# Staging more weights in the second pass of an input projection, and moving half of a weight transform into a later stage

## The chip, the cores and the metric

One Trainium2 (trn2) chip, one of its cores. The metric is the device time of one execution in microseconds (us). TensorE is called PE (PEld its weight loads), VectorE DVE, ScalarE ACT, GpSimd POOL, SyncE SP. DMAs are issued from SP's queue and from ACT's queue.

## The reference

One layer of a bidirectional encoder block, 2048 tokens of 1024 channels, all in float32:

```python
h = rmsnorm(x, g_mix)
p = h @ w_in                                    # 512 Fourier columns, 3 x 512 Hyena columns
y_f = rmsnorm(fourier_mix(p[..., :512]), g_fourier)
y_h = rmsnorm(hyena_mix(p[..., 512:], ...), g_hyena)   # short convolution of 3, two gated long ones
x = x + concat([y_f, y_h]) @ w_out
a = square(relu(rmsnorm(x, g_mlp) @ w_fc1))     # 1024 -> 4096
x = x + a @ w_fc2                               # 4096 -> 1024
out = rmsnorm(x, g_final)
```

## The kernel before

**Products.** Each float32 operand is split into a high part (a cast, on ACT) and a low part (the difference, on DVE or POOL): `split`, lines 178 to 185. A product is then three matmuls (`mm3`, lines 187 to 191): high by high (L189), high by the weights' low part (L190), low by high (L191). The MLP is computed with seven products of half size instead of eight (Strassen's scheme in Winograd's form), `m1` to `m7`; for that, four of the operands on w_fc2's side are sums or differences of its quarters.

**The order of the work.** The kernel is written as one program for all engines. A scheduler places each engine's instructions in a fixed order beforehand: what comes earlier in the program goes first, and an instruction that is ready by its estimates may be placed ahead of earlier ones that aren't. At run time each engine and each queue keeps that order, and an instruction that waits holds what stands behind it. This holds for a DMA too: it waits in its queue, SP's or ACT's, until its buffer is free.

**The input projection, two passes** (`project`, L308). The 16 tiles of tokens (128 tokens each) go through w_in twice, each time for two groups of 512 columns (`sets`). The first pass makes two Hyena groups. It loads x (`fetch`, into buffers with the tag "xt", 2 of 1024 columns), transposes each tile on PE, splits it and writes the transposed tile to a scratch tensor `xtd` (L335). The second pass (`uf` given) makes the Fourier group and the third Hyena group. It reads the tiles from `xtd` (L339) with a DMA on SP's queue, splits them into `xh` and `xl`, and multiplies: 24 matmuls for each of the two groups, 48 per tile. The Fourier result goes to `uf` (L368, ACT), the Hyena result through the short convolution (L374 and L393 on DVE, L397 and L401 on POOL) and out to `gd` (L394, SP).

`weights_in` (L291) brings in the 16 slices of weights of a pass, 8 of each group, 128 x 512 each: load into a staging buffer (L300), split into `wh` and `wl`. In the second pass the staging buffers are the four with the tag "st". The slices of the first group come from the scratch tensor `wfd` and their low parts are made by DVE and POOL in turns (L182); those of the second group are scaled by `g_mix` and their low parts are made by DVE (L185).

**What runs beside the second pass** (`tables`, L1260, taken in turns with `project`, one step per tile). It loads tables for later stages, among them `ff`, two tiles of which use the tag "xt" and four the tag "st". And it makes the sums of w_fc2 (`second_weights`, L1244): for each of 16 pairs of row blocks, f and f + 16, one load of 1 MB (L1251, SP), four subtractions of 128x512 on DVE (L1253 to L1256), and one store of 1 MB to the scratch tensor `td` (L1257, SP). Two rooms in a buffer that is still free there (`f2`) take turns. There are two pairs per step.

**The output projection** (`project_out`, L791). For each tile of tokens: the rows of the Fourier part `yf` are read (L752, L754), both halves are normalised (L815) and transposed (`front`), multiplied by w_out and added to x (`back`, L831, `x2` stored at L832), normalised again (`rows_up`: `hm`, L839) and transposed; every second tile, `combine` makes the sums of the MLP's first operand on POOL (L850 to L853). Beside it the first weights of w_fc1 are loaded (`fc1_weights`, L925) into the four slots of `rp`, a buffer with the tag "W", and their sums and splits are made (L948 to L951, POOL). In the program that stands in step 11 and step 16 of the loop; in the trace the four loads go out at the start of the stage.

Of the kernel before, what the change touches and what calls it, by code (L numbers as in the profile page):

```python
# [134 lines left out]
def hybrid_block(ctx: ExitStack, tc: tile.TileContext, A, out):  # L135
# [155 lines left out]
    def weights_in(wp, sets, stage):  # L291

        w = {}
        for h, s in enumerate(sets):
            src = wfd if s < 0 else A["w_in"][:, (1536, 512, 1024)[s] : (1536, 512, 1024)[s] + 512]
            for k in range(8):
                hi, lo = (wp.tile([P, 512], FR, tag=f"{n}{h}{k}", name=f"{n}{h}{k}") for n in ("wh", "wl"))
                pl, tag, bufs = stage[(8 * h + k) % len(stage)]
                t = pl.tile([P, 512], F32, tag=tag, name="st", bufs=bufs)
                nc.sync.dma_start(t, src[128 * k : 128 * k + 128, :])  # L300
                if s < 0:
                    split(hi, lo, t, None, nc.gpsimd if k % 2 else None)
                else:
                    split(hi, lo, t, gmix[:, k : k + 1])
                w[h, k] = hi, lo
        return w

    def project(ip, fx, cps, sets, uf):  # L308
# [17 lines left out]
        def front(t):  # L326
# [11 lines left out]
            else:  # L338
                nc.sync.dma_start(xc, xtd[t])  # L339
                split(xh, xl, xc)  # L340
# [4 lines left out]
        for i, t in enumerate(order):  # L345
            xh, xl = ahead
            if w is None:
                fetch(1)
                stage = [(fx, "st", 4)] * 4
                if uf is None:  # L350

                    stage += [(cps[h], f"{tag}_{h}", bufs) for h in range(2) for tag, bufs in (("acc", 3), ("m0", 2)) for _ in range(bufs)]
# [436 lines left out]
    tokens = [8 * blk + j + 4 * h for blk in range(2) for j in range(4) for h in range(2)]  # L789

    def project_out(op, work, rp, b):  # L791

# [63 lines left out]

        fronts, old, left = [front(t) for t in tokens[0:3]], None, None
        early = {}
        for i in range(NT + 1):
# [32 lines left out]
            if 2 <= i < NT - 1:  # L892
                fronts.append(front(tokens[i + 1]))
            if i == 1:
                gml = load(op, "gml", [P, 1024], A["g_mlp"].broadcast_to([P, 1024]))
# [338 lines left out]
    with pool("ip") as ip, pool("cp1") as cp1:  # L1234
# [8 lines left out]

        def second_weights(room):  # L1244


            rows = A["w_fc2"].rearrange("(h f p) d -> p h f d", h=2, p=P)
            room = room.rearrange("p f c -> p (f c)").rearrange("p (n h d) -> p n h d", n=2, h=2)
            for f in range(16):
                t = room[:, f % 2]  # L1250
                nc.sync.dma_start(t, rows[:, :, f, :])  # L1251
                b11, b12, b21, b22 = (t[:, h, 512 * e : 512 * e + 512] for h in range(2) for e in range(2))
                nc.vector.tensor_sub(b11, b12, b11)  # L1253
                nc.vector.tensor_sub(b12, b22, b12)
                nc.vector.tensor_sub(b22, b22, b11)
                nc.vector.tensor_sub(b21, b21, b22)  # L1256
                nc.sync.dma_start(td[:, f], t.rearrange("p h (e d) -> p (h e) d", e=2))  # L1257
                yield

        def tables():  # L1260
# [4 lines left out]
            f2, emb = (pl.tile([P, 32, P], F32, tag=n, name=n) for pl, n in ((tp, "f2"), (ep, "emb")))  # L1265
            second = second_weights(f2)
            got.append(load(tp, "e1z", [P, 2, P], A["e1z"]))
            got.append(load(ep, "wo", [P, 2, 512], A["filt_wo"]))
            got.extend((emb, f2))
            for f in range(0, 32, 8):  # L1270
                next(second)
                yield
                next(second)
                nc.sync.dma_start(emb[:, f : f + 8], embd[:, f : f + 8])

            for f in (1, 5, 9, 11, 13, 15):
                next(second, None)
                yield
                next(second, None)
                n = 4 if f < 9 else 2  # L1280
# [96 lines left out]
```

## Time and profile before

| | us |
|---|---|
| median of 3 runs | 2337.66 (2329.79 to 2342.43) |
| the profiled execution | 2342.11 |
| its span | 2340.2 |
| granted PE clock, mean | 0.986 |
| PE busy in the span | 2247.7 |
| DVE, ACT, POOL busy | 1548.4, 1104.3, 846.8 |

A row of the order in time has start, duration, engine, line, operation, output and inputs, and in brackets how long the engine stood before it and what ended that. A matmul's duration reaches to its modelled end, so that matmuls overlap: what they cost is the distance of their starts. In a group's row stand the count, the busy time, the mean duration in ns, and the idle time before them by what ended it.

### The profile page before, as it was taken

Reading aid. Unit: us, or ns where it says so; the run is one execution under the profiler, and the core shown is the slowest. Engines: PE = TensorE matmul, PEld = TensorE weight load, DVE = VectorE, ACT = ScalarE, POOL = GpSimd, SP = SyncE. Lnnn points to the kernel's source line nnn. Section 1 sums busy time; section 2 is a strip of 40 time slices with the busy share of each in tenths; the row PEclk is TensorE's granted clock in tenths of the full one; section 3 lists DMA queues with packets and bytes.
Section 4 is the critical chain, followed back from the end, with each engine's and each line's share of the span. In section 5 each row is a group of like instructions: output and inputs, shape, how many; then the busy total and the mean of one; then the engine's idle time right before and its main releaser. Section 6 shows DMA issues by size and latency. Waiting matters only on the chain.

```text
span 2340.2 us, 30973 instructions
## 1 busy us (share of the span) xinstructions
PE 2247.7 (96%) x10984; PEld 1861.0 (80%) x10984; DVE 1548.4 (66%) x2284; ACT 1104.3 (47%) x1809; POOL 846.8 (36%) x634
## 2 busy tenths in 40 slices
PE   8999998989899989998999999999999999999998
PEld 6887787788788857886788877888888888888886
DVE  7998666789767874447544456444466666866667
ACT  6554211455455554545655566555543333533334
POOL 4345322566656622216755565555400000000000
PEclk9999999999999989999999999999999999999999
DMA  7535888456688986557544456444479766866631
GB/s 258 178 134 179 304 321 300 139 174 206 227 207 191 212 224 189 176 175 244 162 150 149 152 207 203 153 149 151 151 261 377 238 197 196 280 209 197 192 123 72
DMA packets 294779, 468.41 MB, mean 200 GB/s; under 512 B 18453, under 2 KB 142687, under 8 KB 290273
## 3 DMA queue, kind: packets, MB, share of 16 engines
q1 hardware_dynamic: 291265, 460.43, 61.5%
q10 hardware_dynamic: 3360, 6.02, 0.8%
q8 instruction: 86, 1.41, 0.3%
q14 instruction: 68, 0.56, 0.1%
HBM read 312.54 MB, written 152.27 MB: 199 GB/s over the span
## 4 chain that ended last, share of the span: by engine, by line
PE 73%; DMA 9%; DVE 9%; ACT 3%; POOL 3%; issue 2%; SPq 1%; ACTq 0%; DVEq 0%; POOLq 0%
PE p2u L190 5%; PE p2u L189 5%; PE p2u L191 5%; PE p1u L191 5%; PE p1u L189 5%; PE p1u L190 4%; DMA ks<-spec 3%; PE pu L191 3%; PE pu L190 3%; PE pu L189 3%; PE p2v L189 2%; PE p2v L190 2%; PE p2v L191 2%; DMA f<-in_w_fc 2%; PE p1v L189 2%; PE p1v L191 2%
## 5 line engine op out<-in xcount | busy, mean ns | idle before, releaser
L181 ACT CAST qahm<-ra 128x1024 fp32r<-128x1024 f32 x110 | 115.9, 1053 | 345.9 <-PE p2u L190 172.0
L182 DVE TENSOR_TENSOR qalm<-ra,qahm 128x1024 fp32r<-128x1024 f32 x110 | 134.7, 1225 | 155.5 <-ACT qahm L181 151.8
L1159 POOL TENSOR_TENSOR acc<-acc,gfin 128x512 f32<-128x512 f32 x4 | 5.1, 1279 | 633.1 <-DMA out<-acc 625.9
L189 PE MATMUL pu<-wh,xh 128*128 128x512 f32 x512 | 205.7, 403 | 8.9 <-ACT wh L184 5.5
L190 PE MATMUL pu<-wl,xh 128*128 128x512 f32 x512 | 202.6, 396 | 6.5 <-DVE wl L182 3.7
L191 PE MATMUL pu<-wh,xl 128*128 128x512 f32 x512 | 203.0, 397 | 2.7 <-DVE xl L182 2.7
L190 PE MATMUL p2u<-qblm,qahm 128*128 128x512 f32 x504 | 196.2, 389 | 0.5 <-DVE qblm L182 0.5
L189 PE MATMUL p2u<-qbhm,qahm 128*128 128x512 f32 x504 | 195.9, 389 | 0.1
L191 PE MATMUL p2u<-qbhm,qalm 128*128 128x512 f32 x504 | 195.8, 389 | 0.0
L182 DVE TENSOR_TENSOR qblm<-rb,qbhm 128x1024 fp32r<-128x1024 f32 x110 | 134.1, 1219 | 1.4 <-ACT qbhm L181 1.1
L397 POOL TENSOR_TENSOR acc<-acc,cw 128x512 f32<-128x512 f32 x45 | 60.8, 1351 | 202.8 <-DVE acc L374 201.4
L189 PEld LDWEIGHTS pu<-wh,xh 128*128 128x128 f32 x512 | 98.1, 192 | 31.1 <-ACT wh L184 7.0
L181 ACT CAST ahm<-s 128x512 fp32r<-128x512 f32 x124 | 76.6, 620 | 95.3 <-PE p1v L190 55.2
L190 PEld LDWEIGHTS pu<-wl,xh 128*128 128x128 f32 x512 | 98.0, 191 | 28.9 <-DVE wl L182 4.1
L182 POOL TENSOR_TENSOR alm<-W,ahm 128x512 fp32r<-128x512 f32 x63 | 85.9, 1364 | 94.2 <-ACT ahm L181 94.2
L181 ACT CAST qbhm<-rb 128x1024 fp32r<-128x1024 f32 x110 | 115.3, 1049 | 5.0 <-DMA a1m<-c 2.9
L191 PEld LDWEIGHTS pu<-wh,xl 128*128 128x128 f32 x512 | 97.8, 191 | 24.1 <-DVE xl L182 3.6
L189 PEld LDWEIGHTS p2u<-qbhm,qahm 128*128 128x128 f32 x504 | 94.5, 188 | 20.6 <-ACT qbhm L181 0.5
L190 PEld LDWEIGHTS p2u<-qblm,qahm 128*128 128x128 f32 x504 | 94.6, 188 | 20.3 <-DVE qblm L182 1.0
L191 PEld LDWEIGHTS p2u<-qbhm,qalm 128*128 128x128 f32 x504 | 94.6, 188 | 19.8
L191 PE MATMUL p1u<-bm,alm 128*128 128x512 f32 x252 | 100.1, 397 | 6.4 <-DVE alm L182 6.4
L189 PE MATMUL p1u<-bm,ahm 128*128 128x512 f32 x252 | 100.2, 397 | 6.2 <-ACT ku L1022 6.2
(380 smaller groups left out, 6445.4 us busy)
## 6 DMA issues: line engine op xcount, KB each, us to landing
W<-in_w_fc SPq DMA_DIRECT2D x66, 512.0 KB, 4.4
ks<-spec SPq DMA_DIRECT2D x128, 256.0 KB, 6.8
rb<-td SPq DMA_DIRECT2D x64, 512.0 KB, 4.5
ra<-a1m SPq DMA_DIRECT2D x56, 512.0 KB
ra<-a0m SPq DMA_DIRECT2D x54, 512.0 KB, 10.7
rb<-in_w_fc SPq DMA_DIRECT2D x46, 512.0 KB, 4.5
f<-in_w_fc SPq DMA_DIRECT2D x16, 1024.0 KB
td<-f SPq DMA_DIRECT2D x16, 1024.0 KB, 5.0
```

The lines of the kernel that those rows point to most:

```text
L181: nc.scalar.copy(hi, src)
L182: (eng or nc.vector).tensor_sub(lo, src, hi)
L189: nc.tensor.matmul(o, lhsT=lh, rhs=rh, start=start, stop=False, skip_group_check=more)
L190: nc.tensor.matmul(o, lhsT=lh, rhs=rl, start=False, stop=False, skip_group_check=more)
L191: nc.tensor.matmul(o, lhsT=ll, rhs=rh, start=False, stop=stop, skip_group_check=more)
L397: nc.gpsimd.tensor_add(m1, m1, cw[:, 3, :])
L1159: nc.gpsimd.tensor_mul(acc[i][:, c], acc[i][:, c], gfin[:, c])
```

## The change

Three things are changed together.

1. In the second pass the staging buffers are the four "st" buffers and the two "xt" buffers. An "xt" buffer has 1024 columns and takes two slices, which are loaded by one DMA. So eight slices have room at a time instead of four.
2. In the second pass the transposed tokens are loaded from ACT's queue instead of SP's.
3. `second_weights` makes pairs 0 to 7 beside the second pass, one per step instead of two, and pairs 8 to 15 in the output projection, one per step from step 1, in the four slots of `rp`, which `fc1_weights` fills afterwards.

```diff
@@ weights_in
-                t = pl.tile([P, 512], F32, tag=tag, name="st", bufs=bufs)
-                nc.sync.dma_start(t, src[128 * k : 128 * k + 128, :])
+                if tag != "xt":
+                    t = pl.tile([P, 512], F32, tag=tag, name="st", bufs=bufs)
+                    nc.sync.dma_start(t, src[128 * k : 128 * k + 128, :])
+                elif k % 2 == 0:
+                    two = pl.tile([P, 2, 512], F32, tag=tag, name="st2", bufs=bufs)
+                    nc.sync.dma_start(two, src[128 * k : 128 * k + 256, :].rearrange("(a p) d -> p a d", p=P))
+                    t = two[:, 0]
+                else:
+                    t = two[:, 1]
@@ project, front
-                nc.sync.dma_start(xc, xtd[t])
+                nc.scalar.dma_start(xc, xtd[t])
@@ project
                 stage = [(fx, "st", 4)] * 4
-                if uf is None:
+                if uf is not None:
+                    stage += [(fx, "xt", 2)] * 4
+                else:
                     stage += [(cps[h], f"{tag}_{h}", bufs) ...]
@@ second_weights, moved out of the second pass's block
+    def second_weights(room, pairs):
+        rows = A["w_fc2"].rearrange("(h f p) d -> p h f d", h=2, p=P)
+        for f in pairs:
+            t = room[:, f % 2]
+            nc.sync.dma_start(t, rows[:, :, f, :])
+            b11, b12, b21, b22 = (t[:, h, 512 * e : 512 * e + 512] for h in range(2) for e in range(2))
+            nc.vector.tensor_sub(b11, b12, b11)
+            nc.vector.tensor_sub(b12, b22, b12)
+            nc.vector.tensor_sub(b22, b22, b11)
+            nc.vector.tensor_sub(b21, b21, b22)
+            nc.sync.dma_start(td[:, f], t.rearrange("p h (e d) -> p (h e) d", e=2))
+            yield
@@ project_out
+        second = second_weights(rp.rearrange("p (n h) d -> p n h d", n=2), range(8, 16))
...
             if 2 <= i < NT - 1:
                 fronts.append(front(tokens[i + 1]))
+            if 1 <= i:
+                next(second, None)
@@ tables
-            second = second_weights(f2)
+            second = second_weights(f2.rearrange(...), range(8))
             for f in range(0, 32, 8):
                 next(second)
                 yield
-                next(second)
                 nc.sync.dma_start(emb[:, f : f + 8], embd[:, f : f + 8])
             for f in (1, 5, 9, 11, 13, 15):
                 next(second, None)
                 yield
-                next(second, None)
                 n = 4 if f < 9 else 2
```

More of the change, by code (lines that the diff above doesn't have):

```diff
@@ L1242, in hybrid_block @@
         got, ffs = [], []
[L1244 to L1258, printed above, removed]
         def tables():
@@ L1265, in tables @@
             f2, emb = (pl.tile([P, 32, P], F32, tag=n, name=n) for pl, n in ((tp, "f2"), (ep, "emb")))
-            second = second_weights(f2)
+            second = second_weights(f2.rearrange("p f c -> p (f c)").rearrange("p (n h d) -> p n h d", n=2, h=2), range(8))
             got.append(load(tp, "e1z", [P, 2, P], A["e1z"]))
```

## The prediction

> **What bounds the kernel now.** I read the page first, then the windows that cut the span by stage, then the order in time of TensorE (PE), VectorE (DVE) and SyncE's queue (SP) around the two places that the change touches.
>
> ```profile
> span 2340.2 us, 30973 instructions
> PE 2247.7 (96%) x10984; PEld 1861.0 (80%) x10984; DVE 1548.4 (66%) x2284; ACT 1104.3 (47%) x1809; POOL 846.8 (36%) x634
> ```
>
> PE is busy nearly throughout, so only a place where it stands still, or runs at a lower clock, can give time back. The windows say where that is. The columns are the length of the window, busy time of PE, PEld, DVE, ACT and POOL, granted clock, DMA share, GB/s.
>
> ```profile
> 227.00:250.00 23.00, 15.65 (x52) 11.30 (x51) 17.54 (x20) 8.98 (x13) 9.52 (x8) 0.85 0.73 237
> 250.00:365.00 115.00, 114.95 (x507) 94.88 (x506) 78.69 (x96) 20.46 (x24) 34.12 (x22) 1.00 0.87 316
> 365.00:403.00 38.00, 31.86 (x132) 25.27 (x131) 26.77 (x34) 3.47 (x4) 12.64 (x8) 0.96 0.89 327
> 871.00:893.00 22.00, 19.51 (x87) 15.59 (x86) 13.77 (x33) 13.67 (x27) 10.09 (x8) 0.93 0.86 252
> 893.00:945.00 52.00, 51.84 (x257) 43.44 (x256) 25.73 (x85) 24.43 (x61) 10.19 (x8) 1.00 0.55 167
> 945.00:1062.00 117.00, 117.00 (x591) 98.96 (x590) 57.75 (x183) 54.89 (x136) 20.37 (x16) 1.00 0.61 181
> ```
>
> The second pass of the input projection loses time at its beginning (227 to 250: 23.00 - 15.65 = 7.35 us idle, and a clock of 0.85, worth up to 0.15 x 23 = 3.4; I count 3) and near its end (365 to 403: 38.00 - 31.86 = 6.14 idle, 0.04 x 38 = 1.5 of clock). That is 10.4 + 7.6 = 18.0 us, and it is all that the second pass can give: from 250 to 365 PE stands still for 0.05 us. The output projection (871 on) loses 2.5 us idle and 0.07 x 22 = 1.5 of clock in its first 22 us, and after that nothing at all. So work is taken from a stage that has stalls and put into one whose PE has no slack.
>
> **Beginning of the second pass: staging.** What PE waits for there:
>
> ```profile
> 223.83 1.39 SPq L300 DMA_DIRECT2D st<-wfd  x3
> 227.78 1.76 DVE L393 TENSOR_TENSOR acc<-acc,early 128x512 f32<-128x512 f32 x1 [1.46 <-POOL acc L401]
> 229.44 0.39 PE L189 MATMUL pu<-wh,xh 128*128 128x512 f32 x1
> 232.82 1.28 DVE L182 TENSOR_TENSOR wl<-st,wh 128x512 fp32r<-128x512 f32 x2
> 233.34 1.82 SPq L300 DMA_DIRECT2D st<-in_w_in  x4
> 233.55 0.50 PE L190 MATMUL pu<-wl,xh 128*128 128x512 f32 x1 [3.73 <-DVE wl L182]
> 241.18 0.58 PE L190 MATMUL pu<-wl,xh 128*128 128x512 f32 x1 [2.72 <-DVE wl L185]
> 198.74 0.33 SPq L1282 DMA_DIRECT2D ff<-in_ff  x1
> 211.63 0.38 SPq L1282 DMA_DIRECT2D ff<-in_ff  x1
> ```
>
> Sixteen slices of weights go through four buffers. Slices five to eight are fetched only from 223.83, when earlier ones have been split; their split on DVE lands behind three adds of the first pass that begin at 227.78 and end at 232.82, and PE waits 3.73 us. The next four are fetched from 233.34, and PE waits 2.72 us again at 241.18. The two "xt" buffers are free by 198.74 and 211.63: at those times loads of `ff`, which use the same buffers, go out. So all eight slices of the first set can lie in SBUF before 216. DVE has a hole of 1.46 us just before 227.78, and two splits took 1.28 us together, so they can be made there, and the 3.73 us go. They don't all go: the second set is needed 12 products after 229.44, and its first split still stands behind the adds, which end at 232.82. For the rate:
>
> ```profile
> 235.82 0.63 PE L191 MATMUL pu<-wh,xl 128*128 128x512 f32 x1
> 236.25 0.63 PE L189 MATMUL pu<-wh,xh 128*128 128x512 f32 x1
> 256.05 0.39 PE L191 MATMUL pu<-wh,xl 128*128 128x512 f32 x1
> 256.28 0.39 PE L189 MATMUL pu<-wh,xh 128*128 128x512 f32 x1
> 371.97 0.50 PE L191 MATMUL pu<-wh,xl 128*128 128x512 f32 x1 [2.20 <-DVE xl L182]
> ```
>
> Products start 0.23 us apart at full clock (256.05 to 256.28) and 0.43 apart after the stall (235.82 to 236.25). 229.44 + 12 x 0.23 = 232.2, so the second set's first split is 1 to 2 us late, and another 1 us may go where the second set's last four slices wait for the 512-KB buffers. I leave 3 of the 10.4 us and take 7.4 (bounds: 0, if the adds set the pace whatever is staged, and 10.4).
>
> On the lower clock: after the 3.73 us wait products are 0.43 apart, after the 2.20 us wait of 371.97 the row is 0.50 long, not 0.63. The Trainium skill, "TensorE: Matmul & The Clock Gate", what's actually happening, states that about 3.4 us of idleness halve the clock and about 3.4 us of work restore it; this trace agrees with the length of the gap. By that rule short stalls in the output projection would cost only their own length.
>
> **End of the second pass: queue and sums.**
>
> ```profile
> L1253 DVE TENSOR_TENSOR f<-f 128x512 f32<-128x512 f32 x16 | 12.0, 748 | 38.6 <-DMA f<-in_w_fc 38.5
> DVE f L1253 <- DMA f<-in_w_fc: 38.5, 11, 5.3
> 373.81 1.22 DVE L182 TENSOR_TENSOR xl<-xc,xh 128x1024 fp32r<-128x1024 f32 x1
> 389.13 0.60 SPq L339 DMA_DIRECT2D xc<-xt  x1
> 397.02 0.50 PE L189 MATMUL pu<-wh,xh 128*128 128x512 f32 x1 [3.43 <-ACT xh L181]
> 398.73 0.80 PE L191 MATMUL pu<-wh,xl 128*128 128x512 f32 x1 [0.51 <-DVE xl L182]
> 255.40 0.52 ACTq L384 DMA_DIRECT2D nb<-full  x1
> ```
>
> A pair of row blocks of w_fc2 costs DVE four subtractions of 0.75 us, 3.0 us, and in 11 of 16 cases DVE first stood 38.5/11 = 3.5 us for its load. The 2.20 us at 371.97 is a split of tokens behind two such sets. The 3.43 + 0.51 us at 397 are a token load: its buffer was free at 373.81 + 1.22 = 375.0, and SP came to it at 389.13, because it serves loads, stores and sums in a fixed order and waits for each. With eight pairs instead of sixteen the sums end before the last third of the pass, and ScalarE (ACT) issues the load when its buffer is free. I take 7 of the 7.6 us (bounds 3 and 7.6). ACT pays some 16 x 0.52 = 8 us of issuing, beside 20.46 us of work in 115, so nothing. Behind a load that waits for the split of an older token stand ACT's `uf` multiply and the next cast `xh`; the cast has most of a token (48 x 0.23 = 11 us) before PE wants it. I take 0, at worst 2. The Trainium skill, "DMA: Bandwidth & Descriptors", issuing engines are not separate DMA queues, speaks against this part: another issuing engine saves only issue time, since the transfers share the same engines. No row here separates the two, but 14 us of waiting in SP's order are not transfer time.
>
> **Output projection: what comes.** Eight pairs bring 32 subtractions, 32 x 0.75 = 24 us of DVE, and 8 x 2 MB of traffic. DVE has 57.75 busy in 117 and the DMA share is 0.61, so there is room in sum. What counts is when DVE is held, for it has one moment per token:
>
> ```profile
> 945.38 0.68 DVE L831 TENSOR_TENSOR ox<-po,oxt 128x512 f32<-128x512 f32 x1
> 949.77 0.69 DVE L831 TENSOR_TENSOR ox<-po,oxt 128x512 f32<-128x512 f32 x1 [3.72 <-PE po L191]
> 950.83 1.29 DVE L182 TENSOR_TENSOR oyl<-pt_y,oyh 128x512 fp32r<-128x512 f32 x2 [0.36 <-ACT oyh L181]
> 951.79 0.40 PE L191 MATMUL po<-G,oyl 128*128 128x512 f32 x1
> 871.24 7.39 SPq L925 DMA_DIRECT2D W<-in_w_fc  x4
> 889.38 0.66 PE L761 MATMUL pt_y<-turn,oyn 128*128 128x128 f32 x4 [2.25 <-ACT oyn L815]
> ```
>
> The first `oyl` ends at 950.83 + 0.65 = 951.48 and PE reads it at 951.79: 0.3 us of slack. Before that DVE idles 3.72 us, into which 3.0 us of sums fit, if their load has landed. If DVE stands there for the 3.5 us that it stood in the second pass, PE waits 3.2 us. Per pair the cost lies between 0 and 3.2, in sum between 0 and 26. I take 0.4 per pair, 3 us: nearer to the low end, since the hole is larger than the work, and the queue has a share of 0.55 to 0.61 to serve here, against 0.87.
>
> SP's stores `td` and reloads of a room wait in order too, and token rows, `oxt` and the stores of `x2` stand behind them; that is inside these bounds. Two things move with the room: the four `W` loads of fc1, which held SP for 7.39 us at 871.24 ahead of the loads of `yf`, come after the last pair, and two 1-MB loads with short issues take their place. Of the 2.25 us wait at 889.38 and the low clock around it, 4 us in sum, I take 2 back (bounds 0 and 4). The fc1 sums on POOL and their casts then fall among the tokens: 10.09 us of POOL, which is busy 20.37 in 117 there, and ACT's casts ahead of `oyh`; I take 1 us (bounds 0 and 3).
>
> **The sum.** -7.4 - 7 + 3 - 2 + 1 = -12.4 us. The profiled execution took 2342.1 us (span 2340.2), 4.5 above the median of the three runs, 2337.7. From the median: 2337.7 - 12.4 = 2325.3; I say 2325. With every good bound it is -18.0 - 4 = -22, 2316; the runs spread over 12.6 us, and half a per cent (11.7 us) is about what this kernel's measurement can tell from no change.
>
> **Rivals.**
> First, the other side: the sums hold DVE at the token boundary. For it: 0.3 us of slack, and 11 late loads in 16. Against it: a lighter queue. Price: 8 x 3.2 = 26 us; if the clock falls after each stall, 8 products at 0.2 us more are 13 us, of which I count half; with 1 us for fc1 and the gains of 14.4 + 2 that is 26 + 6.5 + 1 - 16.4 = +17: 2355. It decides from a stall of 16.4 / 8 = 2 us per pair; chance 0.25.
> Second, the sums cost PE 1.5 to 2 us per pair, 12 to 16 in sum, and the gain is just given back: 2337; chance 0.15.
> Third, the staging doesn't do what it says: the adds of 227.78 to 232.82 set the pace and the 10.4 us stay. Then -7 + 3 - 2 + 1 = -5: 2333; chance 0.15. For it: the wait of 241.18 is one for DVE, not for a load. Against it: DVE had no slice to split in its hole.
> My forecast keeps 0.45, with a range of its own from 2316 to 2330.
>
> **How the numbers follow.** Faster by over 0.5% is the forecast, 0.45. The second and third rivals lie within 0.5%, 0.30. The first is slower by over 0.5%, 0.25. The range goes from 2313 (all bounds good, and some spread) to 2355, the first rival's middle; what lies above is about half of its 0.25, what lies below a few in a hundred.
>
> **What would show it.** Right: from 227 to 250 PE is over 20 us busy at a clock of 0.95 or more; no idle PE from 365 to the pass's end; the pass ends some 14 us earlier; the loads of `xc` are ACT's; in the output projection's first half PE is idle for under 4 us. Wrong: PE waits for `oyl`, `hm` or `oyh` at token boundaries, DVE's waits for `f` (now "W") are listed with over 2 us each, or the first set's splits still follow 232.

## The result, and the profile after

The changed kernel takes 2348.49 us (median), the kernel before, on the same chip, 2338.52: a ratio of 1.0044 [1.0029, 1.0059]. One run of each kernel was far slower (3758.45 and 12850.81 us) and is left out of the ratio. The changed kernel is slower by 0.44%, about 10 us, where 12 us less was forecast. The profiled execution took 2349.08 us, its span is 2347.3, 7.1 more than before. Nothing was added to the work; there are 30968 instructions, 30973 before:

```profile
PE 2245.1 (96%) x10984; PEld 1858.6 (79%) x10984; DVE 1547.2 (66%) x2284; ACT 1105.1 (47%) x1809; POOL 850.0 (36%) x634
```

In the changed kernel the lines of the second pass lie 10 or 8 higher (L374 is L384, L339 is L347), the sums of w_fc2 are L809 to L812 with their load at L807 and store at L813, and the room is called `W` in the output projection. In the other kernels these numbers lie up to a few lines off. For the ledger by stage, three marks: the first matmul behind the second pass (`pf`), the last matmul of the stage before the output projection (`pb`), and the last matmul of the output projection (`po`). First before, then after; the times are the first and last start.

```profile
L427 PE MATMUL pf<-uf,e1f x32: 592/592/697, 421.2 to 442.9; 128*128 128x512 f32 x32
L678 PE MATMUL pb<-W,b x112: 589/591/1116, 697.9 to 870.6; 128*64 128x512 f32 x112
L191 PE MATMUL po<-V,oyl x128: 387/389/628, 884.5 to 1076.7; 128*128 128x512 f32 x128
```

```profile
L437 PE MATMUL pf<-uf,e1f x32: 592/592/697, 412.6 to 434.3; 128*128 128x512 f32 x32
L688 PE MATMUL pb<-W,b x112: 589/591/1116, 690.8 to 862.9; 128*64 128x512 f32 x112
L191 PE MATMUL po<-V,oyl x128: 387/389/628, 882.5 to 1087.5; 128*128 128x512 f32 x128
```

The second pass ends 421.2 - 412.6 = 8.6 us earlier. The output projection, from the last `pb` to the last `po`, took 206.1 us and takes 224.6: 18.5 more. Between the two marks 0.9 is lost, behind the last `po` 3.7 is gained: -8.6 + 0.9 + 18.5 - 3.7 = 7.1, the whole difference of the spans. Below, "pass" is the time of the first `pf` and "output projection" the time between the last `pb` and the last `po`.

The windows of the changed kernel, with the columns of the prediction's table:

```profile
227.00:250.00 23.00, 15.36 (x54) 11.59 (x54) 18.79 (x24) 7.24 (x11) 9.00 (x8) 0.78 0.80 261
365.00:403.00 38.00, 38.00 (x169) 31.50 (x168) 15.82 (x17) 5.23 (x6) 10.62 (x7) 1.00 0.10 36
863.00:885.00 22.00, 16.86 (x69) 13.22 (x66) 17.42 (x39) 10.19 (x21) 0.00 (x0) 0.84 0.98 346
885.00:937.00 52.00, 46.97 (x219) 38.64 (x218) 28.71 (x81) 20.59 (x50) 5.10 (x4) 0.93 0.75 245
937.00:989.00 52.00, 52.00 (x264) 43.73 (x263) 26.12 (x79) 24.12 (x58) 10.19 (x8) 1.00 0.86 278
989.00:1041.00 52.00, 47.12 (x232) 39.14 (x231) 27.25 (x84) 25.52 (x61) 21.26 (x16) 0.97 0.81 236
```

The end of the second pass is clean: 38.00 busy of 38.00, where 6.14 us stood idle. Its beginning is no better than it was: 7.64 us idle at a clock of 0.78, against 7.35 at 0.85. In the output projection, where PE stood idle for 2.65 us in all before, it now does so for some 5 us in each of three of four windows. PE's rows with an idle time of over 1.9 us in these two stages:

```profile
235.40 0.50 PE L190 MATMUL pu<-wl,xh 128*128 128x512 f32 x1 [3.43 <-DVE wl L182]
243.07 0.79 PE L190 MATMUL pu<-wl,xh 128*128 128x512 f32 x1 [4.21 <-DVE wl L185]
879.74 1.97 PE L771 MATMUL pt_y<-ident,oyn 128*128 128x128 f32 x8 [5.14 <-ACT oyn L840]
927.09 0.79 PE L191 MATMUL po<-G,oyl 128*128 128x512 f32 x1 [4.87 <-DVE oyl L182]
993.48 0.66 PE L771 MATMUL pt_y<-ident,oyn 128*128 128x128 f32 x4 [1.91 <-ACT oyn L840]
1012.30 0.50 PE L189 MATMUL po<-G,oyh 128*128 128x512 f32 x1 [2.71 <-ACT oyh L181]
```

The four stalls from 879 on are 5.14 + 4.87 + 1.91 + 2.71 = 14.6 us, against one of 2.25 before: 12.4 more. The lower clock of the windows is worth at most 0.16 x 22 + 0.07 x 52 + 0.03 x 52 = 8.7 us, against 1.5, which covers the rest of the 18.5. The causes differ. The first stall, in the orders of VectorE and ScalarE:

```profile
872.05 0.69 DVE L809 TENSOR_TENSOR W<-W 128x512 f32<-128x512 f32 x1 [0.32 <-DMA W<-in_w_fc]
875.51 0.69 DVE L809 TENSOR_TENSOR W<-W 128x512 f32<-128x512 f32 x1 [0.59 <-DMA W<-in_w_fc]
876.12 0.15 DVE L216 TENSOR_SCALAR v_h<-ssq_h 128x1 f32<-128x1 f32 x1
876.30 0.20 ACT L197 ACTIVATE sq_s<-v_h 128x1 f32<-128x1 f32 x1 [4.67 <-DVE v_h L216]
```

The sums of the first two pairs were placed at the very start of the stage, though the program has them in steps 1 and 2. An op of 0.15 us, `v_h`, stands behind them; ScalarE waits 4.67 us for it, and with it the first `oyn`, and PE. The second stall:

```profile
910.81 5.77 SPq L880 DMA_DIRECT2D b0m<-t  x4
917.31 0.76 SPq L807 DMA_DIRECT2D W<-in_w_fc  x1
925.74 0.69 DVE L809 TENSOR_TENSOR W<-W 128x512 f32<-128x512 f32 x1 [5.01 <-DMA W<-in_w_fc]
```

SyncE's queue stands at four stores of `combine`'s sums, so the pair's load goes out at 917.31; it has landed at 925.74, and VectorE, which has it next in its order, stands 5.01 us with `oyl` behind it. The third is like these two: VectorE stands before another pair, the small ops for `oyn` are placed among that pair's four subtractions, and ScalarE waits for them.

```profile
988.72 0.69 DVE L809 TENSOR_TENSOR W<-W 128x512 f32<-128x512 f32 x1 [3.03 <-DMA b0m<-raw]
992.71 0.72 ACT L840 ACTIVATE oyn<-zz,nw_s 128x512 f32<-128x512 f32 x1 [2.99 <-DVE nw_s L202]
```

The profile names a store of `b0m` there; the subtraction reads only the pair's room, whose load went out at 979.35, so the load is the likelier cause. The last stall is the weights of fc1, which are now loaded late:

```profile
1010.63 1.14 ACT L181 CAST eahm<-W 128x512 fp32r<-128x512 f32 x2 [8.07 <-DMA W<-in_w_fc]
```

ScalarE waits 8.07 us to cast them, ahead of the `oyh` that PE wants at 1012.30.

The staging did bring its loads forward: the last slices of the first set go out at 199.53 and 211.33, before from 222.13 on. But the work behind them did not get early enough. The changed kernel, ScalarE, VectorE and GpSimd:

```profile
219.36 1.05 ACT L181 CAST xh<-xc 128x1024 fp32r<-128x1024 f32 x1 [6.34 <-DMA xc<-xt]
223.30 5.18 DVE L182 TENSOR_TENSOR wl<-st,wh 128x512 fp32r<-128x512 f32 x3
221.53 6.40 POOL L182 TENSOR_TENSOR wl<-st,wh 128x512 fp32r<-128x512 f32 x4 [1.21 <-ACT wh L181]
234.67 0.68 DVE L182 TENSOR_TENSOR wl<-st,wh 128x512 fp32r<-128x512 f32 x1
```

The casts of the slices stand behind a token load that came late on ScalarE's queue. Then VectorE and GpSimd split at the same time, and a split takes 5.18 / 3 = 1.73 us on VectorE and 6.40 / 4 = 1.60 on GpSimd; the fourth on VectorE, alone at 234.67, takes 0.68. It missed its place, came behind the adds, and PE waits for it at 235.40.

### The profile page after: what moved, and what is told of

Same layout as the page of the kernel before. It is cut to its first block, busy times and chain, and to the rows that moved or that the text cites. A ratio compares the mean times of both kernels' runs of the same rounds, so it can differ in the third digit from the quotient of the medians.

```text
span 2347.3 us, 30968 instructions
## 1 busy us (share of the span) xinstructions
PE 2245.1 (96%) x10984; PEld 1858.6 (79%) x10984; DVE 1547.2 (66%) x2284; ACT 1105.1 (47%) x1809; POOL 850.0 (36%) x634
## 4 chain that ended last, share of the span: by engine, by line
PE 50%; DVE 1%; DMA 1%; ACT 1%; issue 0%; POOL 0%; SPq 0%; DVEq 0%; ACTq 0%; POOLq 0%
PE p2u L189 5%; PE p2u L190 5%; PE p2u L191 5%; PE p1u L191 5%; PE p1u L189 5%; PE p1u L190 5%; PE p2v L189 2%; PE p2v L190 2%; PE p2v L191 2%; PE p1v L189 2%; PE p1v L191 2%; PE p1v L190 2%; PE p2m L189 1%; PE p2m L190 1%; PE p2m L191 1%; PE p1m L189 1%
## 5 line engine op out<-in xcount | busy, mean ns | idle before, releaser
L181 ACT CAST ahm<-W 128x512 fp32r<-128x512 f32 x94 | 57.6, 615 | 104.1 <-PE p1u L190 96.2
```

Source lines behind the costliest of these rows:

```text
L181: nc.scalar.copy(hi, src)
```

## The experiments

Theory at the outset: the 18.5 us are VectorE held by late loads and badly placed sums (H). Rivals: SyncE's order and the traffic (S), the 24 us of VectorE's work (W), and, for the second pass, that one or the other of the three parts does all of it.

| kernel | median | ratio to before | pass ends | output projection |
|---|---|---|---|---|
| before | 2338 to 2340 | 1 | 421.2 | 206.1 |
| changed | 2348.49 | 1.0044 [1.0029, 1.0059] | 412.6 | 224.6 |
| sums moved alone | 2350.33 | 1.0051 [1.0034, 1.0068] | 411.9 | 222.1 |
| staging and ACT's queue alone | 2340.65 | 1.0016 [1.0002, 1.0030] | 420.2 | 204.3 |
| changed, tokens on SP | 2346.75 | 1.0031 [1.0016, 1.0046] | 411.3 | 227.2 |
| changed, sums on POOL | 2353.03 | 1.0064 [1.0041, 1.0088] | 411.8 | 227.9 |
| pairs from step 3 | 2338.18 | 1.0005 [0.9993, 1.0016] | 414.2 | 216.2 |
| transfers without sums | 2336.20 | 0.9995 [0.9985, 1.0005] | 412.6 | 212.8 |
| sums without transfers | 2336.24 | 0.9998 [0.9986, 1.0010] | 411.9 | 211.2 |
| fourteen pairs and two | 2344.16 | 1.0025 [1.0011, 1.0039] | 422.3 | 209.5 |
| sums in VectorE's hole | 2349.34 | 1.0045 [1.0028, 1.0061] | 412.1 | 219.3 |
| and one room | 2347.40 | 1.0043 [1.0028, 1.0057] | 413.5 | 221.3 |
| step 3, gated | 2336.34 | 0.9986 [0.9975, 0.9998] | 412.5 | 212.6 |
| pairs in fc1 | 2374.87 | 1.0156 [1.0142, 1.0170] | 410.8 | 206.9 |
| gated, casts later | 2335.79 | 0.9985 [0.9974, 0.9995] | 412.7 | 212.5 |
| gated, splits on VectorE | 2335.73 | 0.9987 [0.9976, 0.9999] | 410.3 | 212.2 |
| both | 2332.91 | 0.9975 [0.9961, 0.9988] | 408.8 | 212.5 |

The ratios are to the kernel before on the same chip; the medians come from several chips. The last two columns are read from one profiled execution each. Nine kernels whose second pass is written as in the changed kernel end it between 410.8 and 414.2. Those with the output projection as before take 204.3 to 206.9 for it (three kernels), and those with it as in the changed kernel 222.1 to 227.2 (three). Differences of that size show nothing.

### Which part does what

**The sums moved alone**: parts 1 and 2 are undone.

```diff
-                if uf is not None:
-                    stage += [(fx, "xt", 2)] * 4
-                else:
+                if uf is None:
...
-                nc.scalar.dma_start(xc, xtd[t])
+                nc.sync.dma_start(xc, xtd[t])
```

> Part 3 alone: half of the sums go to the output projection; staging (four buffers) and token loads (SP's queue) are as before. Theory (the loss is made in the output projection, where DVE in its fixed order is held by late loads of the pairs, and the gain of the changed kernel comes from the end of the second pass, where the sums no longer run): the second pass ends 7 to 9 us earlier than before, the output projection costs 15 to 20 us more, in sum 2344 to 2350 us, as slow as the changed kernel. Rival (staging and ACT's queue made the changed kernel's gain in the second pass): the second pass ends less than 4 us earlier and the time is above 2352.

The pass ends at 411.9 and the output projection takes 222.1: the moved sums make both the gain in the second pass and the loss in the output projection. With the tokens still on SyncE's queue PE is busy 38.00 us of 38.00 from 365 to 403, and the staging and ScalarE's queue, which the changed kernel has beside the moved sums, bring nothing more (412.6).

**Staging and ACT's queue alone**: all sixteen pairs stay in the second pass, two per step.

```diff
-            if 1 <= i:
-                next(second, None)
...
-            second = second_weights(..., range(8))
+            second = second_weights(..., range(16))
                 next(second)
                 yield
+                next(second)
```

> Parts 1 and 2 alone: staging in six buffers and token loads from ACT's queue, all 16 pairs of sums in the second pass as before. Theory: the output projection is as before; at the beginning of the second pass little is gained (0 to 3 us), because DVE's adds of the first pass set the pace and the casts of the weights start later behind ACT's token load; at the end the wait for the token load goes (3 to 5 us): 2332 to 2337 us. Rival (staging costs time by itself): 2340 or more.

A miss: 1.0 us in the pass, and nothing in the time (2340.65, a ratio of 1.0016). The stall at the beginning stays. Those at 397, laid to the token load in SyncE's order, are gone, and others came:

```profile
235.33 0.50 PE L190 MATMUL pu<-wl,xh 128*128 128x512 f32 x1 [3.39 <-DVE wl L182]
364.52 0.50 PE L191 MATMUL pu<-wh,xl 128*128 128x512 f32 x1 [2.44 <-DVE xl L182]
DVE f L809 <- DMA f<-in_w_fc: 35.6, 13, 6.5
```

VectorE still waits 35.6 us for the pairs' loads (38.5 before), with the splits of tokens behind it.

**The changed kernel with the tokens on SP**, the one line of part 2 undone:

```diff
-                nc.scalar.dma_start(xc, xtd[t])
+                nc.sync.dma_start(xc, xtd[t])
```

> The changed kernel with the token loads of the second pass back on SP's queue. Theory (the load of the pass's first tokens comes later on ACT's queue, 212.1 instead of 207.7, and holds the casts of the weights until 220.3 instead of 216.8): the casts start 3 us earlier, the first wait for a weight's low part at the beginning of the pass falls below 1 us, the pass ends 3 to 7 us earlier than in the changed kernel: 2341 to 2346 us. Rival (the adds of the first pass alone set the pace): the pass ends within 1.5 us of the changed kernel's, 2347 to 2350 us.

The pass ends 1.3 us earlier, not 3 to 7, as the rival had it. That lies inside the spread of the same pass, so neither a cost nor a gain of ScalarE's queue is shown. The stalls at the beginning stay (PE waited 2.3 and 4.6 us).

### What the output projection pays for

**The sums on GpSimd**, in the output projection only:

```diff
-            nc.vector.tensor_sub(b11, b12, b11)
+            (eng or nc.vector).tensor_sub(b11, b12, b11)    # eng: nc.gpsimd; the other three likewise
```

> The changed kernel with the 32 subtractions of the output projection on POOL instead of DVE; loads and stores are the same. Theory (DVE held by late loads is what PE waits for): of the some 18 us that the output projection costs more, at most 6 are left, PE no longer waits for oyl, and the time is 2332 to 2338 us. Rival (the traffic, SP's order of waits and the later fc1 weights make the loss, whichever engine subtracts): 10 us or more are left, 2342 us or more.

My theory in its first form falls. No wait of PE for `oyl` of over 1 us is left, and yet the output projection is no shorter (227.9 against 224.6). SyncE stands instead, at the stores, until GpSimd has made the sums, and the rows of `yf` come late:

```profile
955.30 0.63 ACT L214 ACTIVATE oyn<-yf 128x512 f32<-128x512 f32 x1 [12.63 <-DMA yf<-yfd]
958.54 1.12 PE L771 MATMUL pt_y<-turn,oyn 128*128 128x128 f32 x4 [5.16 <-ACT oyn L840]
```

**Pairs from step 3.**

```diff
-            if 1 <= i:
+            if 3 <= i:
                 next(second, None)
```

> The changed kernel with one edit: the eight pairs of the output projection are made in steps 3 to 10, not 1 to 8. In the changed kernel the first two pairs' subtractions lie on DVE at 872 to 878.5, ahead of the small ops that ScalarE's first token multiply needs, and PE then waits 5.14 us for oyn with some 1.5 us of lower clock behind it. If the place of the first pairs is what costs there, the output projection (last pb to last po, 224.6 us) falls to about 218 and the kernel to about 2342. Rival, the pairs cost what they cost wherever they stand: it stays at 222 to 226 and the time within 2 us of 2348.

8.4 us less in the output projection, some 10 in the time: the kernel is level with before. The size is as expected, the reason isn't: at the start PE waits longer than in the changed kernel, since the first two pairs were again placed ahead of `v_h`.

```profile
879.52 0.69 DVE L809 TENSOR_TENSOR W<-W 128x512 f32<-128x512 f32 x1 [0.79 <-DMA W<-in_w_fc]
883.75 1.97 PE L771 MATMUL pt_y<-ident,oyn 128*128 128x128 f32 x8 [7.00 <-ACT oyn L840]
```

What went are the stalls of 927 and 1012. VectorE waits for the pairs' loads nearly as long as in the changed kernel (12.3 us against 15.1), but most of the waits fall where PE has work; one stall for `oyl` is left, 2.38 us at 993.94.

**Transfers without sums, and sums without transfers.** Both compute something else. The first loads and stores the eight pairs and leaves them unsummed. The second makes all the sums, but loads only the first two pairs and stores only the last two; the other places of `td` are filled with other pairs' rows by added stores in the second pass.

```diff
+            if pairs[0] == 0:                # only in the second pass
                 nc.vector.tensor_sub(b11, b12, b11)
...
```

```diff
-            nc.sync.dma_start(t, rows[:, :, f, :])
+            if f < 10:
+                nc.sync.dma_start(t, rows[:, :, f, :])
...
-            nc.sync.dma_start(td[:, f], ...)
+            for g in {4: (4, 10, 8), 5: (5, 11, 9), 6: (6, 12), 7: (7, 13)}.get(f, () if 8 <= f < 14 else (f,)):
+                nc.sync.dma_start(td[:, g], ...)
```

> The changed kernel without the 32 subtractions of the output projection's eight pairs: each pair is loaded and stored again as it is, so half of the blocks stay unsummed. All DMA traffic, all of SyncE's order, and the late weights of fc1 stay. Output projection before 206.1 us, changed 224.6. Theory H, a late load holds DVE and that is the price: 209 to 213, since only the late fc1 weights are left. Theory S, SyncE's queue and the rooms' order are the price: 218 or more. Theory W, DVE's work of 24 us is the price: 209 or less.

> The changed kernel with the 32 subtractions of the output projection, but only the first two pairs are loaded and only the last two stored there; the subtractions between run again on what lies in the room, so those blocks are not w_fc2's (their places in memory are filled with other pairs' rows from the second pass, which gives that pass 6 MB more of stores; so only the output projection is read). Output projection before 206.1 us, changed 224.6. Theories H and S (late loads, or SyncE's order): 210 to 215, what is left being the first two pairs' place and the late fc1 weights. Theory W (DVE's work itself): 218 or more, and PE still waits for oyl.

The transfers alone cost 6.7 us, the sums alone 5.1, both together 18.5. PE's largest stall with the transfers alone, and with the sums alone:

```profile
994.79 0.80 PE L189 MATMUL po<-G,oyh 128*128 128x512 f32 x1 [3.43 <-ACT oyh L181]
```

```profile
878.62 1.97 PE L771 MATMUL pt_y<-ident,oyn 128*128 128x128 f32 x8 [6.63 <-ACT oyn L842]
```

Sums whose data are there are placed at once: six of the eight pairs were begun between 870 and 893, ahead of and around `v_h`, and that start is the one stall of size. So some 24 us of VectorE's work cost 5.1 even with that start, which is against W. The transfers alone keep the late weights of fc1 and their stall. What is over, 18.5 - 6.7 - 5.1 = 6.7, needs both: sums that wait for their loads would be that, though no run isolates it, and the 18.5 itself has a spread of some 2.5 us to either side.

**Fourteen pairs and two**, on the kernel before: two pairs in each of the first four steps of the pass, one in each of the next six, two in the output projection.

```diff
             for f in (1, 5, 9, 11, 13, 15):
                 next(second, None)
                 yield
-                next(second, None)
...
+            if i in (3, 6):                  # project_out, range(14, 16)
+                next(second, None)
```

> A version that may beat both: the kernel before with fourteen of the sixteen pairs in the second pass (two in each of the first four steps, one in each of the next six, so the second one is dropped only where PE stood still), and the other two in steps 3 and 6 of the output projection; staging and the tokens' queue as before. Second pass: its end at 412 to 415 (before 421.2), if one pair a step in the last six steps is what frees it. Output projection, if the price goes by the pair (16 to 18 us for eight): 206 + 4 = 210, and the kernel 2334 to 2336 against 2339. Rival, the price is one of the late fc1 weights and of the order as a whole: 214 or more, and the kernel 2339 to 2343.

A miss in the pass, which ends at 422.3, and as expected in the output projection, 3.4 us for two pairs. These two were placed ahead of `v_h` as well, and PE's one stall of size there is the wait for the first `oyn`, 4.79 us at 886.93. One pair a step at the end of the pass is still one that holds VectorE:

```profile
368.45 0.69 DVE L807 TENSOR_TENSOR f<-f 128x512 f32<-128x512 f32 x1 [5.88 <-DMA f<-in_w_fc]
376.89 0.79 PE L191 MATMUL pu<-wh,xl 128*128 128x512 f32 x1 [4.79 <-DVE xl L182]
```

So it isn't only the second pair of a step that stalls the end; one a step does so too. In the changed kernel the last pair's sums begin at 317.74.

### Moving the sums in VectorE's order

**Sums in VectorE's hole**: `hole` holds the additions of token rows, two for each step, and `issue_after` fixes an order within the engine without a wait.

```diff
+                hole.append(nc.vector.tensor_add(x2[:, cols], p, xt[:, cols]))
...
+            with tc.issue_after(hole[-2].ins):
                 nc.vector.tensor_sub(b11, b12, b11)
...
```

> The changed kernel with one thing changed in the order of VectorE's instructions, and no work or transfer removed: the four subtractions of each pair of the output projection may be issued only behind the first addition of that step's token rows, which is where VectorE stood idle for 3.72 us before the second addition in the kernel before. Theory H (the price of the pairs is VectorE held at the wrong moment: by the first pairs ahead of the small ops for oyn, and by late loads): the output projection falls from 224.6 us to 208 to 213 and the kernel to 2334 to 2339. Theory S (SyncE's order and the traffic): it stays above 216. The late weights of fc1 stay in both, worth 2 to 4 us.

The stall of 5.14 us at the start is gone (1.08 us are left), and 219.3 us are 5.3 less, not 12 to 17; the kernel is no faster than the changed one (a ratio of 1.0045 against 1.0044). The hole isn't free: the small ops and `hm` of the token before go through it, and PE's transposition of `hm` stands behind them.

```profile
894.56 1.74 PE L224 MATMUL pt_m<-ident,hm 128*128 128x128 f32 x8 [2.97 <-DVE v_h L216]
```

**And one room**, so that fc1's first weights are loaded early:

```diff
-        second = second_weights(rp.rearrange(...), range(8, 16))
+        second = second_weights(rp.rearrange(...)[:, 1:2], range(8, 16), hole, kept)
...
+            with tc.issue_after(kept[-2].ins):    # kept: the stores of x2
                 nc.sync.dma_start(t, rows[:, :, f, :])
```

> As the version with the subtractions in VectorE's hole, and beside it all eight pairs use only one room, that of fc1's second pair of weights, so that fc1's first weights are loaded before the output projection again, as in the kernel before; each load of a pair is issued behind the store of the token rows of the step before, so it has some 8 us to land. If the late fc1 weights cost 2 to 4 us: the output projection 205 to 210 us, the kernel 2331 to 2336 against 2338 before. Rival: one room serialises store, load and subtractions, the loads land late and hold VectorE at the additions, and it is no better than with two rooms (212 or more).

The rival holds. The stall for `oyh` is gone, but each load now waits on SyncE for the store of the same room, with `yf` behind it, and VectorE waits up to 9.8 us for one. The wait lists of SyncE and VectorE (in sum, times, longest), and PE's worst:

```profile
SPq L808 <- DMA td<-W: 13.5, 7, 3.6
DVE W L811 <- DMA W<-in_w_fc: 15.9, 5, 9.8
929.42 1.11 PE L771 MATMUL pt_y<-turn,oyn 128*128 128x128 f32 x4 [4.65 <-ACT oyn L842]
```

**Step 3, gated**: pairs from step 3, each behind the second addition of two steps before.

```diff
-            if 1 <= i:
+            if 3 <= i:
                 next(second, None)
...
+            with tc.issue_after(hole[-5].ins):
                 nc.vector.tensor_sub(b11, b12, b11)
...
```

> The changed kernel with the pairs of the output projection in steps 3 to 10, and each pair's subtractions issued only behind the second addition of the token rows of two steps before; so the first pair can no longer stand ahead of the small ops for the first oyn (a stall of 5.1 us in the changed kernel and of 7.0 where the pairs were only started at step 3), and the others stand where the order puts them. If that place is the largest single price: no stall over 2 us before 900, the output projection 206 to 210 us (216.2 where only the step was changed), and the kernel 2330 to 2335, faster than before. Rival, the price only moves, as it did when all pairs were put into VectorE's hole (219.3): 214 or more and the kernel 2337 or more.

The start is mended: the first `oyn` comes in time, and PE stands nowhere over 0.5 us before 900. The output projection takes 212.6, 12.0 less than in the changed kernel (not the 206 to 210 expected) and 3.6 less than without the gate, which is no more than the spread, though the stall of 7.00 us is gone; and the time is below that of before, by 0.14% [0.02, 0.25]. Two stalls are left:

```profile
977.51 0.69 DVE L810 TENSOR_TENSOR W<-W 128x512 f32<-128x512 f32 x1 [5.28 <-DMA W<-in_w_fc]
981.26 0.50 PE L191 MATMUL po<-G,oyl 128*128 128x512 f32 x1 [2.75 <-DVE oyl L182]
1009.75 0.50 PE L189 MATMUL po<-G,oyh 128*128 128x512 f32 x1 [3.56 <-ACT oyh L181]
```

**Pairs in fc1**: the eight pairs in pieces of 96 columns, two per step of fc1's loop, loaded and stored from SyncE.

```diff
+        for f in pairs:
+            for c in range(0, 512, 96):      # load, four subtractions, store
...
         for i in range(33):
+            for _ in range(2 if 2 <= i < 30 else 0):
+                next(second, None)
```

> The changed kernel with the eight pairs taken out of the output projection and made in fc1's loop, where the kernel before shows PE without idle time, DVE busy 46 of 100 us and a DMA share of 0.47: in pieces of up to 96 columns (1.5 KB of a partition, what was free there), two a step, each loaded, summed and stored from SyncE. fc1's first weights are loaded early again. If the price of the pairs is that the output projection's engines and queues stand in a tight order with PE, and not the work: the output projection is back at 204 to 207 us, the second pass keeps its 8.6, fc1 (636 to 638 us) gains at most 2, and the kernel takes 2329 to 2333 against 2338. Rival: SyncE waits there for each piece's store, fc1's weights come late behind it, and fc1 grows by 6 us or more; then 2336 or more.

Both halves came. The output projection is back at 206.9, and fc1 grows by 46.7 us: from the last `po` to the first matmul of fc2 it takes 684.8 us, not 638.1. There too VectorE waits for the loads of the sums (34 times), and PE for ScalarE's `ku` (39.3 us in 17 times); that the one makes the other was not tested.

```profile
DVE w L826 <- DMA w<-in_w_fc: 83.2, 34, 5.1
```

### What was still open

**Gated, casts later**: fc1's first weights in step 13, their casts behind the last scaling of token rows.

```diff
-            if i == 11:
+            if i == 13:
...
+                    with tc.issue_after(scaled[-1].ins):
                         split(*early[n], src, None, nc.gpsimd)
```

> As the version with the gated pairs (output projection 212.6 us), and fc1's first weights are loaded, summed and cast from step 13 on, not 11, and ScalarE's casts of them may be issued only behind the last scaling of token rows of the step before. If the casts, which waited 8.07 us for late weights ahead of an oyh, are the stall of 3.56 us at 1009.75: the stall goes, the output projection 208 to 210 and the kernel 2331 to 2334 (2336.3 without this edit). Rival: the wait moves to the first products of fc1 or to another cast, and the time stays within 2 us of 2336.

The stall at 1009.75 goes, so the casts were its cause; but the output projection stays at 212.5, since the stall before it grew from 2.75 to 4.55 us, and the clock fell behind it. The windows from 937 to 989 of the gated kernel and of this one (in its next window, 989 to 1041, PE is busy 52.00 us of 52.00):

```profile
937.00:989.00 52.00, 48.96 (x247) 40.77 (x246) 35.05 (x97) 24.79 (x60) 11.29 (x8) 1.00 0.94 302
```

```profile
937.00:989.00 52.00, 47.20 (x223) 38.85 (x222) 33.07 (x93) 24.42 (x60) 11.36 (x8) 0.93 0.95 302
```

The earlier stall is the pair's load again, in a stretch where the transfers' share is 0.95. By the two orders in time it grew because PE came to it 1.3 us earlier while the pair's load had landed only 0.5 us earlier (977.05 against 977.51), and because the pair's second subtraction then ran beside GpSimd's sums and took 1.64 us instead of 0.69. That is read from the traces; no run tests it.

**Gated, splits on VectorE**, for the first set of the second pass:

```diff
-                    split(hi, lo, t, None, nc.gpsimd if k % 2 else None)
+                    split(hi, lo, t)
```

> As the version with the gated pairs, and all eight splits of the second pass's first set are VectorE's, none GpSimd's. In the changed kernel the two engines split at once and a split takes 1.7 us on VectorE, not 0.65, so the fourth falls behind the adds. If that is why the staging gained nothing: eight splits of 0.65 us from 223.3 end at 228.5, the wait of 3.43 us at 235.40 goes, and the pass ends 3 to 5 us earlier (412.5 without this edit), the kernel 2331 to 2334. Rival, the adds of the first pass set the pace whatever is staged: the eight splits are spread among the adds, the pass ends at 411 to 414 or later, and the kernel stays within 2 us of 2336.

Each theory has part of it. A split takes 1.88 / 3 = 0.63 us, and the first stall falls from the gated kernel's 3.98 to 0.95 us. But two of the eight still come behind the second group of adds, where PE waits 4.89 us for them, and the pass ends 2.2 us earlier, not 3 to 5, which alone would hardly be clear of the spread:

```profile
229.46 1.88 DVE L182 TENSOR_TENSOR wl<-st,wh 128x512 fp32r<-128x512 f32 x3
230.19 0.50 PE L190 MATMUL pu<-wl,xh 128*128 128x512 f32 x1 [0.95 <-DVE wl L182]
237.61 1.28 DVE L182 TENSOR_TENSOR wl<-st,wh 128x512 fp32r<-128x512 f32 x2
```

**Both edits** of the last two, on the gated kernel:

> Both edits together, on the version with the gated pairs. If both causes are as said: the second pass ends at 408 to 410, the output projection takes 208 to 210, and the kernel 2328 to 2331 against 2338 before. If only the casts hold: 2331 to 2334. If neither: 2336.

2332.91 us, 0.25% below before [0.12, 0.39]: the lowest time of the kernels run here. The gain on the gated kernel is made in the second pass (408.8, clear of the spread), not by the casts. The output projection is where it was (212.5), its loss now in one stall of 5.49 us at 980.89, behind a load for which VectorE stood 6.01 us.

## Why the prediction was wrong

**The sums in the output projection, +3: the step that failed.** With the -2 for the start of the stage and the +1 for the fc1 weights, the output projection should have lost 2 us; it lost 18.5. The step set 3.0 us of sums per pair against a hole of 3.72 us per token and asked only whether the load would be there. Three things are wrong with that, by the runs. The first pairs were not put into a hole at all: they lie ahead of the stage's first small op. The hole isn't idle for PE's purposes either: with the sums held in it the stage still cost 13.2 us more than before, and the new stalls came through `v_h` and `hm`, where the price had been worked out from the row of `oyl` alone. And the late load, which I left to the upper bound, did come: five of eight pairs waited for it, three of them for over 4 us; 0.4 us per pair was the good case. The start at step 3 gives 8.4 of the 18.5 back and the gate, which only fixes the pairs' place, by these profiles 3.6 more. All three signs of being wrong that the prediction named were there: waits for `oyl` and `oyh`, VectorE's waits for `W`, and a split of the first set behind 232 (at 234.67).

```profile
DVE W L809 <- DMA W<-in_w_fc: 15.1, 5, 5.0
```

**The start of the output projection, -2: wrong in sign.** The loads of fc1's weights did leave it, but what took their place on VectorE made the stall there longer, 5.14 us against 2.25. **The fc1 weights among the tokens, +1: too small.** I counted GpSimd's work and ScalarE's casts, not the 8.07 us that a cast waits for weights that can be loaded only when the last pair has left its room. It is a stall of 2.7 to 3.6 us, and shown to be the casts', though taking it away alone brought nothing in sum.

**The staging, -7.4: nothing of it came.** The third rival was right here: with all loads out early, the two stalls are 3.43 + 4.21 us, where they were 3.73 + 2.72. The step gave VectorE's hole of 1.46 us two splits at 0.64 us, the rate of two splits in a row. They are made beside GpSimd's, at 1.73 us. The trace before has that price as well, for the two splits of the same set that are made beside two of GpSimd's, 3.47 / 2 = 1.73 us; I read the cheap pair at 232.82 and not this one:

```profile
220.88 3.47 DVE L182 TENSOR_TENSOR wl<-st,wh 128x512 fp32r<-128x512 f32 x2
```

That is a cause beside the adds, worth 2.2 to 3.9 us (the pass's end from 412.5 to 410.3, and from 412.7 to 408.8). What is left stands behind the adds: in both kernels PE still waits 4.9 us for splits that come after their second group. (The first of slices five to eight was fetched at 222.13, not 223.83, which changes nothing.)

**The end of the second pass, -7: right in size, wrong in half of its reason.** All the idle time is gone. It is the missing pairs: moving them alone gives 9.3 us, the staging and the token loads without that 1.0. **ScalarE's queue, 0, at worst 2:** the 1.3 us measured do not stand out of the spread. With the token loads on ScalarE's queue and all pairs kept, VectorE waited 35.6 us for its pairs, against 38.5, and the pass gained 1.0 us, not the time of the wait in SyncE's order that I had counted on. The Trainium skill, "DMA: Bandwidth & Descriptors", issuing engines are not separate DMA queues, states that another issuing engine saves only issue time. These runs agree with that.

**The clock.** The gated kernel's stall of 2.75 us left the clock at 1.00 in the window around it, the 4.55 us of the kernel with later casts lowered it to 0.93. So far that agrees with the 3.4 us of the Trainium skill, "TensorE: Matmul & The Clock Gate", what's actually happening. But shorter gaps lowered it too. Behind the 2.25 us at 889.38 in the kernel before, products from 891.54 on take 0.63 us, and behind the 1.91 us at 993.48 in the changed kernel two do, at 996.56 and 996.99; at full clock they take 0.39. So the length of the gap does not settle it here, and the conclusion drawn from it, that short stalls cost only their own length, does not hold for these two, which both lie beside transpositions. Why is open.

**The chances.** The forecast had 0.45. The first rival, VectorE held by the sums (0.25), came nearest in mechanism and in time: it put 2355 us where 2348 were measured, and it was to decide from 2 us per pair, where 18.5 / 8 = 2.3 were paid. It was not right in its terms: it counted on 16.4 us of gains, and took the price to be one wait repeated eight times. The runs show four stalls with differing causes, each of which can move.

## What to carry to other kernels

Side work put into a stage whose main engine has no slack is not priced by its busy time against the idle time of the engine it runs on: here some 24 us of sums with their data at hand cost 5.1 us, their transfers alone 6.7, and the two together 18.5. Ask of each moved instruction what stands behind it in its engine's order and in its queue, above all the small ops of 0.15 us, and look where it is really issued, for work that is ready early is placed early. If it must be there, fix its place behind the critical small ops; here a start two steps later, which gave most of it, and that together turned 0.44% slower into 0.14% faster.

## What the runs showed of the hardware

A subtraction of 128x512 with both inputs in SBUF takes 0.63 us on VectorE alone and 1.73 us while GpSimd makes the like at 1.60. Seven splits shared by the two took from 221.53 to 223.30 + 5.18 = 228.48, 6.95 us; VectorE alone would need 7 x 0.63 = 4.4, an estimate. The Trainium skill, "SBUF — State Buffer", who interferes with whom, states that a VectorE instruction with two SBUF inputs contends with a GpSimd instruction that reads SBUF; the trace agrees. Here the second engine made it slower.

A pair's load of 1 MB, issued at 917.31, had landed at 925.74: 8.4 us in a window with a DMA share of 0.75.
